# Activation tiles moved 64 bytes against the weight tiles in a transformer kernel of one core

## The chip, the core and the metric

The kernel runs on one core of one Trainium2 chip. The time is the time on the device in microseconds (us), from the runs of the whole program; lower is better. The profile is one further execution, taken by the hardware profiler, with its own time. TensorE (PE in the rows) multiplies: it loads a stationary operand of up to 128 columns (PEld in the rows) and streams a moving operand past it. VectorE is DVE, ScalarE is ACT, GpSimd is POOL, and SyncE (SP) issues most of the DMAs. SBUF is the on-chip memory that TensorE reads both operands from; an address below is the byte in each of its 128 partitions at which a tile starts.

## What is computed

Two transformer models one after the other on 256 tokens of width 1024. The first is a block of a mixer (gated delta rule and a state-space layer), a cross attention and a gated feed-forward; the second has two layers, each of a self attention, a small cross attention on a memory, and a feed-forward with a short convolution. Cut to the feed-forward of the first block and the rule of every projection:

```python
def _swiglu(hn, w_gate, w_up, w_down):
    return (jax.nn.silu(hn @ w_gate) * (hn @ w_up)) @ w_down

def conv_ffn(h, w_up, conv_w, conv_b, w_down):
    u = h @ w_up                                  # [256, 2 * 2816]
    ...
    return (jax.nn.silu(gate) * val) @ w_down

def reference(...):
    x = first_block(x, mem, ...)
    return second_block(x, mem_2, positions_2, ...)
```

All inputs are float32, and each of the 1024-wide weight matrices is used once.

## The kernel before

**The products.** A float32 product is made of three products in the format fp32r: each operand is split into a high part and a low part, and the kernel adds high x high, high x low and low x high. `mm3` (lines 533 to 536) does this for the projections, `out_mm` (lines 574 to 582) for the products that add into the residual. In `proj_f` the stationary operand is a 128x128 piece of the weights (`whi`, `wlo`) and the moving one 256 columns of the activations (`xh`, `xl`); in `proj_t` (lines 545 to 553) the two change sides. In `out_mm` the weights are stationary and `oh`, `ol` or the two halves of `ahl` move. So every matmul of these lines has a weight load of 128 columns and a moving operand of 256 columns, both of 4 bytes.

**Weights on their way.** `Weights` (lines 45 to 185) loads 512 KB of a matrix at a time on the SP queue (line 101) into a `raw` tile. ScalarE copies it to `whi` (line 137), VectorE subtracts to get `wlo` (line 157), and the load that comes next may then use the `raw` tile. There are four `raw` tiles and four pairs of `whi`, `wlo` in the pool `weights`, three more pairs in the pool `weights2`, which is opened at line 1682, and from line 1685 on two extra load tiles (`raw4`) in the pool `main`. Of 336 loads of line 101, 136 land in `raw4`.

**Where the tiles lie.** Pools are placed one behind the other, and the tiles of a pool one behind the other, each rounded up to 32 bytes. In the built program before the change the order is `const`, `weights` (from byte 7808), `main` (from 56960), `small`, then `mixer` and later `second` in its place (from 119296), and `weights2` (from 196352). All of `weights`, `main` and `weights2` and nearly all tiles of `second` start at a multiple of 128: `whi` and `wlo` of `weights` at 128 past a multiple of 256, those of `weights2` at a multiple of 256, `xh` (69248) and `xl` (77440) at 128 past one, `ahl`, `oh` and `ol` at a multiple of 256. Every step inside these tiles from one matmul to the next is a multiple of 512 bytes. A few tiles lie elsewhere: in `mixer`, the tile `s5ghl` (the gated state-space output, high and low half, from 139200) lies 64 past a multiple of 128, and it moves past `whi` and `wlo` in 48 matmuls of lines 534 to 536; in `second`, `wfs` (from 190656, the 16 gate columns of the second layer, high and low) also lies 64 past one, and it is stationary for `xh` and `xl` in 16 matmuls of lines 564 and 565.

**The order.** The kernel is written with tile pools and a scheduler that fixes each engine's order when the program is built. TensorE works through its matmuls in that order, and the weight load of one matmul runs while the matmul ahead of it streams.

Of the kernel before, what the change touches and what calls it, by code (L numbers as in the profile page):

```python
# [10 lines left out]
F32 = mybir.dt.float32  # L11
# [176 lines left out]
def behind(tc, later, earlier):  # L188

    tc.add_manual_dep(later, earlier.name, mybir.DependencyInfo(  # L190
        mybir.DependencyClass.NoSync, mybir.DependencyReason.DATA), reason="order")
# [38 lines left out]
def body(ctx, tc, I, out):  # L230
# [7 lines left out]
    main = ctx.enter_context(tc.tile_pool(name="main", bufs=1))  # L238
    small = ctx.enter_context(tc.tile_pool(name="small", bufs=2))
    W = Weights(nc, wpool, 4, 4, lambda a, b: behind(tc, a, b))  # L240


    def cols(w, c0, c1):
        return w.rearrange("(k p) n -> p k n", p=128)[:, :, c0:c1]

    def rows(w, r0, n=2):
        return w[r0 * 128:(r0 + n) * 128].rearrange("(k p) n -> p k n", p=128)
# [3 lines left out]
    for nm in "ukqvz":  # L251
        for c in range(2):
            W.add((nm, c), cols(w_in, OFFS[nm] + 256 * c, OFFS[nm] + 256 * c + 256), split=nm not in "uk")
            for x, at in enumerate(XK_AT):
                if at == (nm, c):
                    W.add(("xk", x), cols(I["w_xk"][0], 256 * x, 256 * x + 256))
    W.add("glu", I["s5_w_glu"][0].rearrange("(k p) n -> p k n", p=128), "k")
    for c in (2, 3, 0, 1):
        W.add(("out", c), rows(I["w_out"][0], 2 * c), "k")
    for i in range(4):  # L260
        W.add(("xq", i), cols(I["w_xq"][0], 256 * i, 256 * i + 256), order=False)
        W.add(("xv", i), cols(I["w_xv"][0], 256 * i, 256 * i + 256), "k", order=False)
        W.add(("xo", i), rows(I["w_xo"][0], 2 * i), "k", order=False)
# [1416 lines left out]
    residual(accs, COL["ffn"])  # L1680
    px_cm.__exit__(None, None, None)
    W.more = (ctx.enter_context(tc.tile_pool(name="weights2", bufs=1)), 3)
    padded = ctx.enter_context(tc.tile_pool(name="padded", bufs=1))
    W.nextra = 2
    W.extra = lambda: main.tile([128, 2048], F32, name="raw4", tag="m8", bufs=3)
# [496 lines left out]
```

## Time and profile before

| | |
|---|---|
| median of 3 runs | 1225.01 us |
| lowest and highest of them | 1219.74 and 1227.4 us |
| the profiled execution's own time | 1218.84 us |
| its span, first to last instruction | 1217.1 us |
| mean granted TensorE clock | 0.99 of full speed |
| TensorE matmuls busy | 1180.5 us (97%), 9720 instructions |
| TensorE weight loads busy | 1127.1 us (93%), 9720 |
| VectorE, ScalarE, GpSimd busy | 893.4, 667.1, 77.6 us |

A matmul's busy time runs from its start to a modelled end, and the next one starts before that end, so busy time adds up overlaps. What one matmul costs in a stream is the time from its start to the start of the next; it is read from the rows of the timeline.

### The profile page before, as it was taken

To read this page: it belongs to the slowest core of one execution; us is meant where nothing else is said; L and a number is where in the kernel's file an instruction comes from. 1 tells how busy PE (TensorE), PEld (TensorE's weight loads), DVE (VectorE), ACT (ScalarE), POOL (GpSimd) and SP (SyncE) were. 2 spreads that over 40 slices of the span, in tenths; PEclk is the share of its full clock that TensorE was granted. 3 is DMA by queue.
4 is the path that set the end of the run, shared out by engine and by line. 5 is a ranking of instruction groups with operands and counts; after the bars stand their busy time and mean duration, and the time that the engine had idled before them with its cause. 6 is when DMAs were issued, how large, how long until landed. Compare 5 with 4: busy or idle time off the path is not lost.

```text
span 1217.1 us, 24101 instructions
## 1 busy us (share of the span) xinstructions
PE 1180.5 (97%) x9720; PEld 1127.1 (93%) x9720; DVE 893.4 (73%) x1682; ACT 667.1 (55%) x1155; POOL 77.6 (6%) x175
## 2 busy tenths in 40 slices
PE   7899998999999999999998999999999999999998
PEld 6799888999999999997897999999988888999998
DVE  8799747766775656787776888777665676977775
ACT  5554345755544444655666665555454666655553
POOL 1426300100000000300000000000100000000000
PEclk9999899999999999999999999999999999999998
DMA  8733353647655655743352665765543454566520
GB/s 211 187 93 104 87 161 107 184 152 194 192 177 175 206 174 148 219 144 121 112 158 90 187 179 174 211 188 156 140 139 117 145 158 135 174 188 193 174 87 35
DMA packets 262017, 188.01 MB, mean 154 GB/s; under 512 B 20143, under 2 KB 246852, under 8 KB 261906
## 3 DMA queue, kind: packets, MB, share of 16 engines
q1 hardware_dynamic: 258034, 185.23, 51.4%
q8 instruction: 76, 1.25, 0.4%
q10 hardware_dynamic: 3568, 0.86, 0.3%
q0 software_dynamic: 304, 0.39, 0.3%
q14 instruction: 35, 0.29, 0.1%
HBM read 183.70 MB, written 2.75 MB: 153 GB/s over the span
## 4 chain that ended last, share of the span: by engine, by line
PE 88%; DVE 4%; DMA 3%; ACT 2%; issue 1%; POOL 1%; SPq 0%; ACTq 0%; DVEq 0%; POOLq 0%
PE mm L534 17%; PE mm L535 17%; PE mm L536 17%; PE acc L580 7%; PE acc L582 7%; PE acc L581 7%; PE mm L1377 2%; DMA raw<-in_w_in_dram 1%; PE acc L1991 1%; PE acc L1862 1%; DMA D<-d 1%; DVE wlo L157 1%; DMA raws<-in_w_out_dram 1%; PE mm L2045 1%; PE mm L1578 0%
## 5 line engine op out<-in xcount | busy, mean ns | idle before, releaser
L137 ACT ACTIVATE whi<-raw 128x1024 fp32r<-128x1024 f32 x322 | 337.1, 1057 | 319.0 <-PE mm L535 114.8
L157 DVE TENSOR_TENSOR wlo<-raw,whi 128x1024 fp32r<-128x1024 f32 x322 | 392.4, 1227 | 162.0 <-ACT whi L137 159.7
L534 PE MATMUL mm<-xh,whi 128*128 128x256 f32 x1504 | 427.0, 285 | 2.1 <-ACT V L218 1.2
L535 PE MATMUL mm<-xl,whi 128*128 128x256 f32 x1504 | 425.7, 283 | 0.0
L536 PE MATMUL mm<-xh,wlo 128*128 128x256 f32 x1504 | 425.4, 283 | 0.0
L534 PEld LDWEIGHTS mm<-xh,whi 128*128 128x128 f32 x1504 | 286.3, 191 | 4.2 <-ACT V L218 1.4
L535 PEld LDWEIGHTS mm<-xl,whi 128*128 128x128 f32 x1504 | 286.7, 191 | 1.4 <-issue 1.1
L536 PEld LDWEIGHTS mm<-xh,wlo 128*128 128x128 f32 x1504 | 286.8, 191 | 0.3
L582 PE MATMUL acc<-ahl,wlo 128*128 128x256 f32 x528 | 146.4, 282 | 0.4 <-DVE wlo L157 0.4
L581 PE MATMUL acc<-ahl,whi 128*128 128x256 f32 x528 | 146.4, 282 | 0.0
L580 PE MATMUL acc<-ahl,whi 128*128 128x256 f32 x528 | 143.3, 282 | 0.0
L582 PEld LDWEIGHTS acc<-ahl,wlo 128*128 128x128 f32 x528 | 99.2, 189 | 0.7 <-DVE wlo L157 0.6
L581 PEld LDWEIGHTS acc<-ahl,whi 128*128 128x128 f32 x528 | 99.4, 189 | 0.0
L580 PEld LDWEIGHTS acc<-ahl,whi 128*128 128x128 f32 x528 | 97.3, 189 | 0.3 <-ACT ahl L218 0.2
L1736 DVE SCALAR_TENSOR_TENSOR gu<-pad,cwc,gu 128x256 f32<-128x256 f32 x176 | 75.3, 480 | 3.4 <-ACT gu L218 3.4
L580 PE MATMUL acc<-oh,whi 128*128 128x256 f32 x224 | 62.5, 288 | 0.9 <-ACT oh L218 0.9
L582 PE MATMUL acc<-oh,wlo 128*128 128x256 f32 x224 | 62.8, 283 | 0.0
L581 PE MATMUL acc<-ol,whi 128*128 128x256 f32 x224 | 62.5, 281 | 0.0
L218 ACT ACTIVATE gu<-pad,cwc 128x256 f32<-128x256 f32 x88 | 47.5, 589 | 13.9 <-DVE pad L745 13.9
L745 DVE TENSOR_TENSOR pad<-mm,rb 128x512 f32<-128x512 f32 x44 | 30.2, 689 | 20.1 <-PE mm L536 20.1
L580 PEld LDWEIGHTS acc<-oh,whi 128*128 128x128 f32 x224 | 41.3, 188 | 2.5 <-ACT oh L218 1.9
L582 PEld LDWEIGHTS acc<-oh,wlo 128*128 128x128 f32 x224 | 42.1, 188 | 1.1 <-issue 1.1
(537 smaller groups left out, 1962.7 us busy)
## 6 DMA issues: line engine op xcount, KB each, us to landing
raw<-in_ffn_w_up_dram SPq DMA_DIRECT2D x88, 512.0 KB
raw<-in_ffn_w_down_dram SPq DMA_DIRECT2D x44, 512.0 KB
raw<-in_ab_w_in_dram SPq DMA_DIRECT2D x24, 512.0 KB
raw<-in_fox_w_in_dram SPq DMA_DIRECT2D x24, 512.0 KB
raw<-in_w_gate_dram SPq DMA_DIRECT2D x22, 512.0 KB
raw<-in_w_up_dram SPq DMA_DIRECT2D x22, 512.0 KB
raw<-in_w_down_dram SPq DMA_DIRECT2D x22, 512.0 KB
raw<-in_w_in_dram SPq DMA_DIRECT2D x20, 512.0 KB
```

Source lines behind the costliest of these rows:

```text
L137: i_ = self.nc.scalar.activation(hi, src, AF.Copy)
L157: i_ = self.nc.vector.tensor_tensor(lo, src, hi.bitcast(F32), op=OP.subtract)
L218: i = self.nc.scalar.activation(out, in_, func, **kw)
L534: T.matmul(p, lhsT=wh, rhs=xh, start=start, stop=False, **kw)
L535: T.matmul(p, lhsT=wh, rhs=xl, start=False, stop=False, **kw)
L536: T.matmul(p, lhsT=wl, rhs=xh, start=False, stop=stop, **kw)
L580: T.matmul(p, lhsT=wh[:, kk, c], rhs=xh, start=first and n % 2 == 0, stop=False, skip_group_check=True)
L581: T.matmul(p, lhsT=wh[:, kk, c], rhs=xl, start=False, stop=False, skip_group_check=True)
L582: T.matmul(p, lhsT=wl[:, kk, c], rhs=xh, start=False, stop=last, skip_group_check=True)
L745: N.v = V.tensor_tensor(o, a, b, op=op).ins
L1377: T.matmul(p, lhsT=w[:, k], rhs=x32[:, k], start=k == 0, stop=k == KD - 1)
L1736: STT(t[:, i], u[:, i, d:d + S], cw(d, j + NH * i), t[:, i], op0=OP.mult, op1=OP.add)
```

## The change

Two tiles of 16 float32 columns (64 bytes in each partition) are allocated and never used: one at the head of the pool `main`, one at the head of `weights2`.

```diff
     W = Weights(nc, wpool, 4, 4, lambda a, b: behind(tc, a, b))
+
+    main.tile([128, 16], F32, name="beside", bufs=1)
 
...
     W.more = (ctx.enter_context(tc.tile_pool(name="weights2", bufs=1)), 3)
+    W.more[0].tile([128, 16], F32, name="beside2", bufs=1)
     padded = ctx.enter_context(tc.tile_pool(name="padded", bufs=1))
```

The first moves every tile that is allocated behind it by 64 bytes: all of `main` (from 57024 now), `small`, `mixer`, `second`, `cross`. The pool `weights` lies ahead of it and stays. `weights2` would be moved by 64 too; the second tile moves its `whi` and `wlo` by 64 more, so that they start at multiples of 128 again (128 past a multiple of 256 now). In the built program `xh` and `xl` start 192 past a multiple of 256, `ahl`, `oh` and `ol` 64 past one, and all `whi` and `wlo` 128 past one: each pair of lines 534 to 536 and 580 to 582 is 64 bytes apart, counted in multiples of 128. The pairs that were 64 apart come to the same place, like `s5ghl` with `whi`; `wfs` moves with `main`'s tiles and stays 64 apart from them. The tiles `raw` stay, `raw4` moves by 64. Each engine's instructions, their order and what each waits for are the same in both programs, line by line.

## Rows read from the trace of the kernel before

**Rows 1.** The page: busy us of each engine, and the chain that ended last.
```profile
span 1217.1 us, 24101 instructions
...
PE 1180.5 (97%) x9720; PEld 1127.1 (93%) x9720; DVE 893.4 (73%) x1682; ACT 667.1 (55%) x1155; POOL 77.6 (6%) x175
...
PE 88%; DVE 4%; DMA 3%; ACT 2%; issue 1%; POOL 1%; SPq 0%; ACTq 0%; DVEq 0%; POOLq 0%
```

**Rows 2.** Busy us (instructions) by stretch; then granted clock, DMA share, GB/s.
```profile
400.00:500.00 100.00, 100.00 (x838) 99.85 (x838) 63.26 (x81) 51.63 (x73) 1.57 (x1) 1.00 0.62 180
700.00:800.00 100.00, 100.00 (x840) 100.00 (x839) 83.08 (x128) 57.66 (x88) 0.93 (x1) 1.00 0.63 186
1100.00:1200.00 100.00, 100.00 (x838) 99.86 (x838) 75.05 (x118) 54.06 (x81) 0.00 (x0) 1.00 0.42 127
```

**Rows 3.** Groups by line, PE: form, count, busy us, mean ns, idle before.
```profile
L534 PE MATMUL mm<-xh,whi 128*128 128x256 f32 x1504 | 427.0, 285 | 2.1 <-ACT V L218 1.2 <-ACT xh L218 0.9
...
L581 PE MATMUL acc<-ahl,whi 128*128 128x256 f32 x528 | 146.4, 282 | 0.0
...
L581 PE MATMUL acc<-ol,whi 128*128 128x256 f32 x224 | 62.5, 281 | 0.0
...
L536 PE MATMUL mm<-whi,xl 128*128 128x256 f32 x128 | 37.0, 289 | 0.0
...
L534 PE MATMUL spare<-memh,whi 128*128 128x256 f32 x64 | 19.5, 304 | 2.4 <-ACT xkT L218 2.4
...
L581 PE MATMUL dn<-xl,whi 128*128 128x256 f32 x32 | 9.0, 283 | 0.0
```

**Rows 4.** Timeline of PE, 301.60 to 303.04 us: start us, duration us, instruction.
```profile
301.60 0.28 PE L534 MATMUL mm<-xh,whi 128*128 128x256 f32 x1
301.72 0.28 PE L535 MATMUL mm<-xl,whi 128*128 128x256 f32 x1
...
303.04 0.28 PE L534 MATMUL mm<-xh,whi 128*128 128x256 f32 x1
```

**Rows 5.** Timeline of PEld, the weight loads, at the same place; columns as in Rows 4.
```profile
301.60 0.19 PEld L535 LDWEIGHTS mm<-xl,whi 128*128 128x128 f32 x1
```

**Rows 6.** Groups by line in that stretch; columns as in Rows 3.
```profile
L534 PEld LDWEIGHTS mm<-xh,whi 128*128 128x128 f32 x5 | 1.0, 192 | 0.0
```

**Rows 7.** Timeline of PE, 750.92 to 753.66 us, 24 matmuls of the down projection.
```profile
750.92 0.28 PE L580 MATMUL acc<-ahl,whi 128*128 128x256 f32 x1
...
751.63 0.28 PE L580 MATMUL acc<-ahl,whi 128*128 128x256 f32 x1
751.76 0.28 PE L581 MATMUL acc<-ahl,whi 128*128 128x256 f32 x1
...
753.66 0.28 PE L582 MATMUL acc<-ahl,wlo 128*128 128x256 f32 x1
```

**Rows 8.** Timeline of PE, 178.63 to 182.28 us, 32 matmuls.
```profile
178.63 0.28 PE L535 MATMUL mm<-s5ghl,whi 128*128 128x256 f32 x1
...
182.28 0.28 PE L535 MATMUL mm<-s5ghl,whi 128*128 128x256 f32 x1
```

**Rows 9.** Timeline of PE, 184.83 to 186.08 us, 12 matmuls.
```profile
184.83 0.28 PE L535 MATMUL mm<-s5ghl,whi 128*128 128x256 f32 x1
...
186.08 0.28 PE L580 MATMUL s<-xh,whi 128*128 128x256 f32 x1
```

**Rows 10.** Timeline of PE, 871.45 to 873.05 us, 15 matmuls.
```profile
871.45 0.28 PE L565 MATMUL acc<-xl,wfs 128*16 128x256 f32 x1
...
871.80 0.28 PE L564 MATMUL acc<-xh,wfs 128*32 128x256 f32 x1
...
873.05 0.28 PE L565 MATMUL acc<-xl,wfs 128*16 128x256 f32 x1
```

**Rows 11.** The tile s5ghl: ns min/median/max, first and last start us.
```profile
L534 PEld LDWEIGHTS mm<-s5ghl,whi x16: 187/188/192, 178.2 to 185.6; 128*128 128x128 f32 x16
...
L218 ACT ACTIVATE s5ghl<-s5g x4: 406/407/408, 177.1 to 178.1; 128x256 fp32r<-128x256 f32 x4
L745 DVE TENSOR_TENSOR s5ghl<-s5g,s5ghl x4: 418/420/425, 177.6 to 178.6; 128x256 fp32r<-128x256 f32 x4
```

**Rows 12.** The tile ahl, the same columns.
```profile
L218 ACT ACTIVATE ahl<-sl x66: 398/401/420, 326.3 to 1198.8; 128x256 fp32r<-128x256 f32 x66
L745 DVE TENSOR_TENSOR ahl<-sl,ahl x66: 415/420/428, 327.5 to 1199.2; 128x256 fp32r<-128x256 f32 x66
```

**Rows 13.** Clock and DMA in the four stretches; columns as in Rows 2.
```profile
178.70:182.30 3.60, 3.60 (x33) 3.60 (x32) 2.21 (x4) 2.00 (x5) 0.00 (x0) 1.00 0.14 19
184.90:186.00 1.10, 1.10 (x12) 1.10 (x12) 0.88 (x3) 1.10 (x3) 0.00 (x0) 1.00 0.00 0
301.60:303.00 1.40, 1.40 (x14) 1.40 (x13) 1.40 (x5) 1.15 (x4) 0.00 (x0) 1.00 0.85 202
871.80:873.00 1.20, 1.20 (x13) 1.07 (x11) 1.17 (x3) 0.00 (x0) 0.00 (x0) 1.00 1.00 329
```

## The prediction

> **What bounds the kernel now.** I read the page first, then the stretches, then single starts. The page [rows 1] shows TensorE busy for 97% of 1217.1 us, and the chain that ended last runs on it for 88%. VectorE is busy for 73%. In three stretches of 100 us out of the feed-forwards TensorE and its weight loads are both busy for all of the time, at full clock, and 838 to 840 matmuls pass in each [rows 2]: one starts 119.3 ns behind the other. VectorE is at 63 to 83% there and the DMA engines at 42 to 63%, so what bounds these stretches is the pace of TensorE itself, and whatever changes that pace changes the time nearly one for one.
>
> So the number to look at is the time from start to start. A projection out of `xh` [rows 4] starts a matmul every 1.44 us / 12 = 120.0 ns. The weight load of the next matmul starts together with it [rows 5] and takes 192 ns [rows 6]. A down projection [rows 7] has 23 steps in 2.74 us, 119.1 ns each, but unevenly: one of them, at 751.63, is 130 ns wide at the timeline's resolution of 10 ns.
>
> Now the same triple of products with `s5ghl` as the moving operand. It has the same form, 256 columns past 128, and the same kind of weights; but `s5ghl` lies 64 bytes beside a multiple of 128 from `whi` and `wlo`, where `xh` and `ahl` lie at a multiple of 128 from them. One stream of it [rows 8] makes 31 steps in 3.65 us, 117.7 ns each. Another, 2.5 us later [rows 9], makes 11 steps in 1.25 us, 113.6 ns each. In the third stream of such pairs, `xh` and `xl` past `wfs` [rows 10], the first three steps take 117 ns (871.45 to 871.80), and the following 11 take 1.25 us again, 113.6 ns each. The weight loads of `s5ghl` take 188 ns at the median [rows 11] against 192. The clock is full in all of these stretches [rows 13]. The DMA engines stand still in the one at 184.9 us and are full in the one at 871.8 us, at the same pace; so the pace does not follow the traffic. What the streams below 118 ns share is the 64 bytes.
>
> **The change part by part.** No instruction comes, goes or moves, so the whole effect is in durations.
>
> *TensorE.* The pairs that change sides are those of lines 534 to 536 and 580 to 582. Counted from rows [rows 3], each line standing for the three of its triple: 3 x 1504 of `xh`, 3 x 528 of `ahl`, 3 x 224 of `oh`, 3 x 128 with the sides exchanged, twice 3 x 64 with `memh` (once with the sides exchanged), and four times 3 x 32 of `mem2h` and of the last projection of the mixer: 4512 + 1584 + 672 + 384 + 384 + 384 = 7920. Their cost now is 119.3 ns a step [rows 2], 945 us together. Their cost behind the change is not in the trace of before, because none of these streams lies 64 apart; the nearest rows are the three streams that do. They bound it: at 113.6 ns each step saves 5.7 ns, 7920 x 5.7 = 45 us; at 117.7 ns it saves 1.6 ns, 7920 x 1.6 = 13 us. Both paces hold for ten steps and more, in one and the same form, and I see nothing in the rows that says which of them a stream falls into. By streams it is two to one for the fast pace; by steps (31 and 3 to 22) it is three to two for the slow one. I take the middle, 115.6 ns: 7920 x 3.7 = 29 us.
>
> *The other way.* The 48 matmuls of `s5ghl` come to a multiple of 128 from their weights. At 120.0 ns against a mean near 116 they lose 48 x 4 ns = 0.2 us. `wfs` keeps its 64 bytes.
>
> *VectorE and ScalarE.* They read and write the moved tiles too. The same two operations on `s5ghl` (64 beside) take 407 and 420 ns at the median [rows 11], on `ahl` (a multiple of 128) 401 and 420 ns [rows 12]. I put nothing down for them; 6 ns on each ScalarE copy would lie beside TensorE's work, since ScalarE is at 52 to 58% [rows 2].
>
> *Cover.* A faster TensorE asks for weights sooner. At 113.6 ns the 100 us stretches last 95 us; VectorE's 83.1 us are then 87% and the DMA share of 0.63 becomes 0.66. The DMA engines have shown a share of 0.85 beside a TensorE that didn't wait [rows 13], so the cover holds, and I take nothing off.
>
> **The sum.** 1218.84 - 29 + 0.2 = 1190 us, from the profiled execution's own time. That execution lies 6 us below the median of the runs, 1225.01; a median of the changed kernel may lie as much above my number.
>
> **The rivals.**
>
> *A, all in the fast pace.* Every stream falls into 113.6 ns as in [rows 9, 10]: 1218.84 - 45 = 1174 us. For it: in [rows 10] the stream goes from the slower pace to the faster and stays. Against: [rows 8] stays slow for 31 steps.
>
> *B, all in the slow pace.* 117.7 ns everywhere: 1206 us. For it: that is the longest of the three streams, and most like the projections. Against: the two others.
>
> *C, no change.* The three streams are faster for a reason of their own, or the place of an operand has no effect. [...] The time would then be 1219 us. What the rows have against it is 192 against 188 ns for a load and 120.0 against 113.6 ns for a step in the same form [rows 4, 6, 9, 11]; what they leave open is whether the 64 bytes did it, for three streams are few. One thing speaks for it: the unevenness of [rows 7] shows that the pace also varies where the distance is a multiple of 128.
>
> *D, slower.* The two readings meet later instead of at the start: with one operand half of 128 bytes ahead, the load catches up with the matmul inside it, and the streams settle at the wide steps that [rows 7] has now and then, say 122 to 125 ns. 7920 x 2.7 to 5.7 ns is 21 to 45 us: 1240 to 1264 us. It decides once the mean step is above 120.8 ns (1% of the time is 12 us, and 12 / 7920 is 1.5 ns). Against it: no pace in [rows 8 to 10] is above 118 ns.
>
> The moved load tiles `raw4` could be written more slowly. The DMA engines would bind only if the share of 0.63 grew to 1, that is, if these 40% of the loads took 2.5 times as long. [...]
>
> **How the numbers follow.** The mixture of both paces: 0.42. A: 0.20. B: 0.15. C: 0.17. D: 0.06. A measurement of this kernel tells about 1% from no change, which is 12 us. Faster by more than that are the mixture, A, and most of B (1206 is 19 us below the median, 13 below the profiled time): 0.42 + 0.20 + 0.13 = 0.75. Within 1%: C and the rest of B, 0.19. Slower: D, 0.06. The range reaches from A at its lower bound with a few us of scatter, 1168, to C at the median of the runs, 1225; it leaves out D and half of C, and a little of A. The likeliest case's own range, with 114.5 to 117 ns a step, is 1180 to 1202.
>
> **What would show it.** The step in the projections, 120.0 ns now, should lie between 113 and 118 ns, and the weight loads of `xh` should take 188 ns instead of 192. The 100 us stretches should hold 850 to 880 matmuls instead of 838. The streams of `s5ghl` should go up to about 120 ns. VectorE's and ScalarE's durations should stay, and their shares rise by the shortening alone. If steps and loads stay at 120 and 192 ns, C holds. If the step falls and the time does not, waits of TensorE for `wlo`, `whi` or `raw` must have grown, and my cover was wrong.

## The result and the profile of the changed kernel

The changed kernel takes 1208.34 us (median of 4 runs, 1203.32 to 1209.01) against 1222.85 us for the kernel before, measured beside it: a ratio of 0.987, with a 95% interval of 0.983 to 0.991. So it is faster, by half of the forecast gain: 14.5 us between the medians and 15.5 us between the profiled executions (1203.32 against 1218.84), where 29 us were forecast.

The page of the changed kernel: its span, the busy us of each engine, and the chain that ended last; these answer to [rows 1].

```profile
span 1201.5 us, 24101 instructions
...
PE 1163.9 (97%) x9720; PEld 1110.1 (92%) x9720; DVE 890.5 (74%) x1682; ACT 667.5 (56%) x1155; POOL 79.5 (7%) x175
...
PE 86%; DVE 5%; DMA 4%; ACT 3%; POOL 1%; issue 1%; SPq 0%; DVEq 0%; ACTq 0%; POOLq 0%
```

TensorE is still the bound, with 16.6 us less of busy time; VectorE's and ScalarE's busy times are within 3 us of those before. The same three stretches as [rows 2], busy us and instructions of PE, PEld, DVE, ACT and POOL, then granted clock, DMA share and GB/s:

```profile
400.00:500.00 100.00, 99.89 (x859) 99.70 (x858) 66.38 (x81) 52.23 (x76) 5.47 (x4) 1.00 0.63 183
700.00:800.00 100.00, 100.00 (x852) 100.00 (x851) 82.68 (x128) 57.96 (x87) 0.93 (x1) 1.00 0.66 189
1100.00:1200.00 100.00, 95.33 (x813) 94.92 (x811) 72.32 (x125) 50.82 (x79) 0.00 (x0) 1.00 0.37 113
```

838 to 840 matmuls have become 852 to 859 (the third stretch now holds the end of the program). Single starts, PE's timeline of the changed kernel at four places (start us, duration us, instruction): a projection out of `xh`, a down projection of the first feed-forward, one of the second, and the stream of `s5ghl`, which the change brought from 64 to 128 bytes past its weights, counted modulo 256 (it starts at byte 139264 now, a multiple of 256, and `whi` at 128 past one).

```profile
338.87 0.28 PE L536 MATMUL mm<-xh,whi 128*128 128x256 f32 x1
...
341.70 0.28 PE L536 MATMUL mm<-xh,whi 128*128 128x256 f32 x1
```

```profile
337.51 0.28 PE L582 MATMUL acc<-ahl,whi 128*128 128x256 f32 x1
...
338.76 0.28 PE L584 MATMUL acc<-ahl,wlo 128*128 128x256 f32 x1
```

```profile
744.60 0.28 PE L584 MATMUL acc<-ahl,wlo 128*128 128x256 f32 x1
...
747.07 0.28 PE L584 MATMUL acc<-ahl,wlo 128*128 128x256 f32 x1
```

```profile
180.48 0.28 PE L536 MATMUL mm<-s5ghl,whi 128*128 128x256 f32 x1
...
182.86 0.28 PE L538 MATMUL mm<-s5ghl,wlo 128*128 128x256 f32 x1
```

The projection makes 24 steps in 2.83 us, 117.9 ns each, where [rows 4] had 120.0. The first down projection makes 11 steps in 1.25 us, 113.6 ns (the timeline rounds to 10 ns; by the trace's starts in whole ns, streams of this pace go at 113.3); the one of the second feed-forward, with the same operands at the same places, 21 steps in 2.47 us, 117.6 ns. `s5ghl` went from 117.7 [rows 8] to 119.0 ns (20 steps in 2.38 us), unevenly, like the down projection of [rows 7], which was 128 apart. So both paces that the prediction had seen are there, and the frequent one is the slow one. The weight loads of the projections went from 192 [rows 6] to 188 ns, and the two operations that make the weights kept their time: 1226 ns against 1227 before, and 1057 in both (page, groups by line: form, count, busy us, mean ns, idle before and its releaser):

```profile
L157 DVE TENSOR_TENSOR wlo<-raw,whi 128x1024 fp32r<-128x1024 f32 x322 | 391.9, 1226 | 151.1 <-ACT whi L137 149.3
L137 ACT ACTIVATE whi<-raw 128x1024 fp32r<-128x1024 f32 x322 | 337.1, 1057 | 299.7 <-PE mm L537 117.3
...
L536 PEld LDWEIGHTS mm<-xh,whi 128*128 128x128 f32 x1504 | 281.8, 188 | 4.2 <-ACT V L218 1.4
```

**Where the time went.** Below, a *step* is the time from the start of an fp32r matmul of 256 columns to the start of the next, where that is below 135 ns (nothing waited). Summed over the trace, before has 7910 steps with a mean of 119.36 ns, 944.2 us; the changed kernel 7904 with 117.06, 925.2 us. Matched one to one, the steps got 18.1 us shorter, and all other time of TensorE 1.8 us longer, 3.4 us of it in the mixer between 117 and 198 us, where the granted clock of the stretch from 100 to 150 us was 0.86 instead of 0.90.

### The profile page after: what moved, and what is told of

It is laid out like the page before. It is cut to its first block, busy times and chain, and to the rows that moved or that the text cites. A ratio compares the mean times of both kernels' runs of the same rounds, so it can differ in the third digit from the quotient of the medians.

```text
span 1201.5 us, 24101 instructions
## 1 busy us (share of the span) xinstructions
PE 1163.9 (97%) x9720; PEld 1110.1 (92%) x9720; DVE 890.5 (74%) x1682; ACT 667.5 (56%) x1155; POOL 79.5 (7%) x175
## 3 DMA queue, kind: packets, MB, share of 16 engines
q8 instruction: 76, 1.25, 0.4%
## 4 chain that ended last, share of the span: by engine, by line
PE 86%; DVE 5%; DMA 4%; ACT 3%; POOL 1%; issue 1%; SPq 0%; DVEq 0%; ACTq 0%; POOLq 0%
PE mm L536 17%; PE mm L537 17%; PE mm L538 17%; PE acc L584 7%; PE acc L582 7%; PE acc L583 7%; DMA raw<-in_w_in_dram 1%; PE acc L1994 1%; DVE wlo L157 1%; PE acc L1865 1%; DMA D<-d 1%; ACT whi L137 1%; DMA raws<-in_w_out_dram 1%; DMA s5u<-uT 1%; PE mm L2048 1%
## 5 line engine op out<-in xcount | busy, mean ns | idle before, releaser
L157 DVE TENSOR_TENSOR wlo<-raw,whi 128x1024 fp32r<-128x1024 f32 x322 | 391.9, 1226 | 151.1 <-ACT whi L137 149.3
L137 ACT ACTIVATE whi<-raw 128x1024 fp32r<-128x1024 f32 x322 | 337.1, 1057 | 299.7 <-PE mm L537 117.3
L536 PE MATMUL mm<-xh,whi 128*128 128x256 f32 x1504 | 422.5, 282 | 2.2 <-ACT V L218 1.2
L537 PE MATMUL mm<-xl,whi 128*128 128x256 f32 x1504 | 421.0, 280 | 0.0
L538 PE MATMUL mm<-xh,wlo 128*128 128x256 f32 x1504 | 420.3, 280 | 0.0
L536 PEld LDWEIGHTS mm<-xh,whi 128*128 128x128 f32 x1504 | 281.8, 188 | 4.2 <-ACT V L218 1.4
L537 PEld LDWEIGHTS mm<-xl,whi 128*128 128x128 f32 x1504 | 281.9, 188 | 1.4 <-issue 1.1
L538 PEld LDWEIGHTS mm<-xh,wlo 128*128 128x128 f32 x1504 | 282.2, 188 | 0.3
L583 PE MATMUL acc<-ahl,whi 128*128 128x256 f32 x528 | 145.1, 279 | 0.0
L582 PE MATMUL acc<-ahl,whi 128*128 128x256 f32 x528 | 141.7, 279 | 0.0
L747 DVE TENSOR_TENSOR pad<-mm,rb 128x512 f32<-128x512 f32 x44 | 30.1, 688 | 18.2 <-PE mm L538 18.1
```

The source lines that it names most:

```text
L137: i_ = self.nc.scalar.activation(hi, src, AF.Copy)
L157: i_ = self.nc.vector.tensor_tensor(lo, src, hi.bitcast(F32), op=OP.subtract)
L536: T.matmul(p, lhsT=wh, rhs=xh, start=start, stop=False, **kw)
L537: T.matmul(p, lhsT=wh, rhs=xl, start=False, stop=False, **kw)
L538: T.matmul(p, lhsT=wl, rhs=xh, start=False, stop=stop, **kw)
L582: T.matmul(p, lhsT=wh[:, kk, c], rhs=xh, start=first and n % 2 == 0, stop=False, skip_group_check=True)
```

## The experiments

The number that orders them is the *distance*: the start of the moving operand, minus the start of the stationary operand that is loaded while it streams (that of the matmul behind), modulo 256. A *pair* is such a moving operand and such a load. Before, `xh` lies at 0 and `ahl`, `oh` at 128 from the weights of the first pool, and the reverse from those of `weights2`. In the changed kernel `xh` lies at 64 and `ahl`, `oh` at 192 everywhere, and nearly all of the few streams in which weights move past activations at 192. All kernels down to the last four below have the instructions, the order and the waits of the kernel before; only the places of the tiles differ. Their edits are given against the kernel before.

### Is it the distance?

Two kernels. The first moves everything, weights too, by 64 bytes; the second moves the activations by 128.

```diff
+    wpool.tile([128, 16], F32, name="beside0", bufs=1)     # e_all64, ahead of the weights
+    main.tile([128, 32], F32, name="beside", bufs=1)       # e_main128, instead
```

> The 64-byte tile stands ahead of the weight tiles, so weights and activations both move by 64 bytes and every distance between the two operands of a matmul is that of the kernel before. Theory 1 (the distance of the two operands sets the step from one matmul to the next): no change, about 1222 us, steps of 120.0 ns in the projections out of xh, loads of 192 ns. Theory 2 (the place of the activations itself, or the moved load tiles, sets it): about 1208 us and steps of 117.7 ns as in the changed kernel.

> Activations moved by 128 bytes instead of 64. xh and xl then lie 128 past a multiple of 256 from the weights, where the down and output projections (ahl, oh) lie now, and these lie at a multiple of 256, where xh lies now. Theory 1a (only the distance within 128 bytes counts): no change, 1222 us. Theory 1b (the distance within 256 bytes counts): the two groups change paces, xh from 119.8 to about 118.5 ns a step and ahl and oh from 118.7 to about 120 ns; 5200 x -1.3 + 2200 x 1.3 ns is -4 us, 1218 us.

Measured: e_all64 1222.58 us, ratio 1.0007 (0.9989 to 1.0025); e_main128 1219.4 us, 0.9959 (0.994 to 0.9978). The stretch from 700 to 800 us, of e_all64 and of e_main128:

```profile
700.00:800.00 100.00, 100.00 (x840) 100.00 (x839) 83.14 (x130) 57.39 (x88) 0.93 (x1) 1.00 0.63 184
```

```profile
700.00:800.00 100.00, 100.00 (x842) 100.00 (x842) 83.42 (x128) 58.17 (x87) 0.93 (x1) 1.00 0.62 190
```

With everything 64 bytes on, but the distances as before, 840 matmuls pass, as in [rows 2]. With `xh` and `ahl` exchanging their distances, they exchange their paces: `xh` at 128 goes unevenly at a mean of 118.74 ns (4604 steps), and a down projection now runs in steps of 120.0, eight of them in 0.96 us, where [rows 7] was uneven at 119.1. PE's timeline of e_main128:

```profile
744.83 0.28 PE L581 MATMUL acc<-ahl,whi 128*128 128x256 f32 x1
...
745.79 0.28 PE L583 MATMUL acc<-ahl,wlo 128*128 128x256 f32 x1
```

So in these two kernels the step went with the distance, not with the place (840 matmuls in the stretch of e_all64, as before) and not with the stream's identity; and 128 is too small a modulus, since `xh` went at 119.79 ns at 0 (before) and at 118.74 ns at 128.

### Which distance

```diff
+    main.tile([128, 48], F32, name="beside", bufs=1)       # e_main192: xh 192, ahl and oh 64 (first pool only)
+    main.tile([128, 8], F32, name="beside", bufs=1)        # e_main32: xh 32, ahl and oh 160
+    W.more[0].tile([128, 24], F32, name="beside2", bufs=1)
+    main.tile([128, 24], F32, name="beside", bufs=1)       # e_main96: xh 96, ahl and oh 224
+    W.more[0].tile([128, 8], F32, name="beside2", bufs=1)
```

> Activations moved by 192 bytes: 64 apart from the weights of the first pool again, but to the other side. In the changed kernel the moving operand lies 64 past the weights in the projections out of xh (steps of 117.7 ns) and 64 ahead of them, in 256 bytes, in the down and output projections (115.9 ns). Here the sides are exchanged. Theory A (the side sets the pace): xh about 115.9 ns and ahl, oh about 117.7 ns a step; against the changed kernel 4000 x -1.8 + 2000 x 1.8 ns, about -4 us, 1204 us less what the second weight pool loses (its pairs lie as in the kernel before: 900 x 1.5 ns, +1 us). Theory B (both sides hold two paces, 117.7 and 113.3 ns, and what enters the stream decides): xh keeps 117.7 ns where it comes from a slow stream; 1208 us.

> Activations moved by 32 bytes, the second weight pool with them so that all weights lie alike: xh 32 past the weights, ahl and oh 160 past (32 past a multiple of 128). Theory 1 with a step at 64 bytes (two places count as one within 64 bytes): as the kernel before, 1222 us, xh at 120 ns. Theory 1 in small steps: half of the gain, xh near 118.8 ns, about 1214 us.

> xh and xl 96 past a multiple of 256 from their weights in both pools, ahl and oh at 224, the exchanged streams at 160. Measured so far: 32 gave 116.8 ns (xh), 64 117.7, 128 118.7, 160 119.0 (ahl) and 118.3 (oh), 192 115.4 to 116.0, 224 118.4 (exchanged), 0 119.8. Theory 1 (a curve that rises from 32 to 160 and has its low point at 192): xh at 118.2, ahl at 118.4, 7900 steps at a mean of 118.2 ns, 9 us less than before: 1210 us profiled. Rival 2 (multiples of 64 alone are special, and 32 and 96 are alike): xh at 116.8, 1203 us.

Measured: e_main192 1202.68 us, ratio 0.9836 (0.9811 to 0.9862); e_main32 1213.49 us, 0.9918 (0.989 to 0.9945); e_main96 1222.52 us, 0.9998 (0.9982 to 1.0015). In e_main192 the two groups exchange the mean paces of the changed kernel, as its theory A had it. The 1214 us that one theory gave e_main32 came out by luck: `xh` went to 116.8 ns where it said 118.8, and `ahl` and `oh`, at 160, hardly got faster. The means of the large groups, from the starts in each trace:

| distance | stream (kernel) | steps | mean ns | at most 114.5 ns |
|---|---|---|---|---|
| 0 | xh (before) | 3978 | 119.79 | 1% |
| 32 | xh (e_main32) | 4576 | 116.81 | 10% |
| 64 | xh (changed kernel) | 4605 | 117.70 | 3% |
| 64 | ahl (e_main192) | 1311 | 117.87 | 1% |
| 96 | xh (e_main96) | 4589 | 119.89 | 0% |
| 128 | ahl (before) | 1311 | 118.81 | 1% |
| 160 | ahl (e_main32) | 1573 | 118.99 | 0% |
| 192 | ahl (changed kernel) | 1573 | 116.00 | 39% |
| 192 | xh (e_main192) | 3955 | 115.43 | 53% |
| 224 | ahl (e_main96) | 1573 | 118.24 | 0% |

The curve that was expected for e_main96 is wrong, and so is its rival: 96 is as slow as 0, and 32 isn't like 96. At 32 the steps are uneven: one stream makes 14 of them in 1.63 us, and the trace's starts in whole ns show 117, 120, 114 and 116 ns again and again, 116.75 at the mean (PE's timeline of e_main32):

```profile
345.33 0.28 PE L536 MATMUL mm<-xl,whi 128*128 128x256 f32 x1
...
346.96 0.28 PE L535 MATMUL mm<-xh,whi 128*128 128x256 f32 x1
```

Of the eight distances of the table, only at 64 and 192 was a stream seen at about 113 ns step after step (11 steps at 64 in [rows 9]; at 192, 11 steps of the first down projection above). Two further kernels ask whether 64 and 192 are two things, or whether what was fast at 192 was fast for another reason: e_both64 puts every stream to 64, and e_shift128 keeps the changed kernel's distances and moves all tiles, weights too, by another 128 bytes, so that each operand's own place modulo 256 is exchanged. (These and all that follow free 256 bytes by a smaller reserve for DMA descriptors.)

```diff
+    main.tile([128, 16], F32, name="beside", bufs=1)       # e_both64
+    pm.tile([128, 32], F32, name="beside1", bufs=1)        #   at the head of the pool second
+    W.more[0].tile([128, 48], F32, name="beside2", bufs=1)
+    wpool.tile([128, 32], F32, name="beside0", bufs=1)     # e_shift128
+    main.tile([128, 16], F32, name="beside", bufs=1)
+    W.more[0].tile([128, 16], F32, name="beside2", bufs=1)
```

> The mirror: every moving tile lies 64 past a multiple of 256 from its weights, in both pools; the streams with the sides exchanged at 192. Theory 1 (64 and 192 are different, and 64 mostly keeps 117.7 ns): xh as in the changed kernel at 117.7 ns, ahl up from 116.0 to 117.9, oh from 115.4 to 116.4 or more, the exchanged ones at 115.8: 1573 x 1.9 + 633 x 1.0 = 3.6 us more than the changed kernel, 1207 us for a profiled run, a mean step of 117.5 ns. Rival 2 (which stream it is decides, not the side): ahl and oh stay at 116.0 and 115.4, 1203 us.

> The changed kernel with all of its tiles, weights too, 128 further on: each distance as in the changed kernel, but the weights at a multiple of 256 instead of 128 past one, xh at 64 past one instead of 192, ahl at 192 instead of 64. Theory 1 (only the distance counts): xh at 117.7 ns, ahl at 116.0, the same time as the changed kernel, 1203 to 1208 us. Rival 2 (the place of the moving operand modulo 256 decides: in the runs so far the fast streams were those whose moving operand lay at 64 past a multiple of 256): xh becomes fast, 115.4 ns, ahl slow, 117.9; 4605 x 2.3 - 1573 x 1.9 = 7.6 us less, 1196 to 1200 us.

Measured: e_both64 1207.96 us, ratio 0.9877 (0.9843 to 0.9911); e_shift128 1202.25 us, 0.9831 (0.981 to 0.9853). The first feed-forward, 70 us out of it, in the changed kernel, in e_shift128 and in e_both64:

```profile
400.00:470.00 70.00, 70.00 (x604) 70.00 (x603) 41.86 (x50) 31.41 (x41) 0.00 (x0) 1.00 0.65 190
```

```profile
400.00:470.00 70.00, 70.00 (x604) 70.00 (x603) 42.22 (x50) 31.55 (x42) 0.00 (x0) 1.00 0.62 189
```

```profile
400.00:470.00 70.00, 70.00 (x597) 70.00 (x596) 41.77 (x50) 31.01 (x42) 0.00 (x0) 1.00 0.64 187
```

e_shift128 repeats the changed kernel to the matmul: 604 and 604 here, `xh` at a mean of 117.70 ns in both, `ahl` at 116.00 in both. So again the step went with the distance alone. In e_both64 `ahl` is slow throughout (117.79 ns, none at 113.3) and the first feed-forward loses its fast down projections, as theory 1 had it; the time is that of the changed kernel within the intervals.

What the two also show is that a choice between the paces can repeat. In the changed kernel a down projection that follows an up projection without a pause took the fast pace in 17 of 19 cases in the first feed-forward, in 0 of 21 in the second and 1 of 21 in the third; in e_shift128 the counts are the same three. The traces also show what fits this, where streams at 192, 64 and 192 followed each other without a wait. The stretch at 64 went at 117.75 ns out of either pace, and yet the stream behind it mostly took up the pace that the one ahead of it had: in the traces of the changed kernel, e_main192, e_shift128 and e_reset_no0 (below), fast to fast 46 times, slow to slow 84 times, slow to fast 3 times, and never fast to slow (stretches of six steps and more, most of them turns of the same loops). So a down projection mostly had the pace of the one before it.

### What chooses between 113.3 and 117.75 ns

The next kernel puts all moving tiles at 192 and leaves no change of distance between up and down projections.

```diff
+    main.tile([128, 48], F32, name="beside", bufs=1)       # e_all192
+    pm.tile([128, 32], F32, name="beside1", bufs=1)
+    W.more[0].tile([128, 16], F32, name="beside2", bufs=1)
```

> Every moving tile (xh, xl, ahl, oh, ol, mem) lies 192 past a multiple of 256 from its weights, in both weight pools; the streams with the sides exchanged then lie at 64. The profiled kernel with only the pairs on the first pool at 192 for xh and 64 for ahl had xh steps of 115.43 ns, and the changed kernel had ahl steps of 116.0 and oh steps of 115.44 ns at 192. Theory 1 (the distance modulo 256 sets which paces a stream may take, and at 192 it falls into 113.3 ns about half of the time): all big classes at 115.4 to 116 ns, 7900 steps at a mean of 115.6, 11 us less than the changed kernel's profiled 1203.3: 1192 us, and no more than a few us given back. Rival 2 (the pace depends on the stretch of the program and its loads, and some streams will run slowly wherever the operands lie): a mean near that of the best so far, 116.4 ns, 1200 us. Rival 3 (a faster TensorE now runs into its loads): steps of 115.6 ns, but more idle time before the first matmul of a stream, 1200 us or more.

Measured: 1201.85 us, ratio 0.9819 (0.9795 to 0.9844). The mean step is 116.05 ns (7903 steps), between theory 1 and rival 2; all other time of TensorE grew by 3.7 us against before, so rival 3 is not what is missing. But the mean hides the finding. Three stretches, one out of each feed-forward:

```profile
400.00:470.00 70.00, 70.00 (x620) 70.00 (x620) 43.75 (x52) 32.20 (x43) 0.00 (x0) 1.00 0.66 196
700.00:800.00 100.00, 100.00 (x852) 100.00 (x851) 81.67 (x124) 56.59 (x84) 0.93 (x1) 1.00 0.64 192
1050.00:1150.00 100.00, 100.00 (x851) 100.00 (x850) 77.14 (x119) 57.32 (x84) 0.00 (x0) 1.00 0.60 179
```

The first feed-forward runs wholly at 113 ns (70 us / 620), the other two wholly at 117.4 (100 us / 852). In the first, 1221 matmuls in a row keep the fast pace; in the third, 1374 keep the slow one. Where the third became slow can be seen: twelve steps at 113.3 ns (1.36 us), then the broadcast of the statistics of line 455, a plain float32 matmul that stands in the trace as two records, 0.59 us together, and from there ten steps of 118 ns (1.18 us). PE's timeline of e_all192:

```profile
1014.33 0.28 PE L535 MATMUL mm<-xh,whi 128*128 128x256 f32 x1
...
1015.69 0.28 PE L535 MATMUL mm<-xh,whi 128*128 128x256 f32 x1
1015.80 0.59 PE L455 MATMUL acc<-diag,ones 128*128 128x256 f32 x2
1016.05 0.47 PE L536 MATMUL mm<-xl,whi 128*128 128x256 f32 x1
1016.35 0.28 PE L537 MATMUL mm<-xh,wlo 128*128 128x256 f32 x1
...
1017.53 0.28 PE L535 MATMUL mm<-xh,whi 128*128 128x256 f32 x1
```

So in this trace a pace held over more than a thousand matmuls (1221 and 1374), and at this one matmul of another form it changed. To test whether an interruption sets the pace and the stream then keeps it, the same kernel gets nine matmuls in the second and third feed-forward, whose result is overwritten by the projection behind them. In e_kick9 they have the sides exchanged, which makes their distance 64, with one pair at 0 on the way in (`xh` streams while `xh` is loaded) and one on the way out (`whi` while `whi` is loaded); in e_kick9_same they are like the projections. The two kernels differ in these rows alone.

```diff
             p = mm()
+            if conv is not None and j == 4:
+                wh, _ = W.get((tag, "g", j // 2), j % 2)
+                for _ in range(9):
+                    T.matmul(p[:, :S], lhsT=N.xh[:, 0, 0:128], rhs=wh[:, 0:2].rearrange("p k c -> p (k c)"), start=True, stop=True)    # e_kick9
+                    T.matmul(p[:, :S], lhsT=wh[:, 0], rhs=N.xh[:, 0], start=True, stop=True)    # e_kick9_same
             proj_f(p[:, :S], (tag, "g", j // 2), j % 2)
```

> The kernel with every moving tile at 192 past its weights, plus nine matmuls each in the feed-forwards of the second model's two layers, ahead of the fifth gate projection, with the sides exchanged (weights move, activations stand: distance 64), whose result the next projection overwrites. Without them the trace shows both feed-forwards in the 117.75 ns pace, 1405 steps from 662.0 to 829.4 us and 1345 from 1020.0 to 1178.9 us, set by the statistics matmuls at their head. Theory 1 (the pace is a state that an entry sets and that holds until something breaks the stream; in the six cases of that kernel where weights had moved at 64 in the 117.75 pace and activations came back at 192, the stream went on at 113.3): behind the nine matmuls the steps fall to 113.3 ns and stay: some 2650 steps x 4.4 ns = 11.7 us, less 18 x 0.118 = 2.1 us for the added matmuls: about 9.5 us less than without, 1186 us profiled, median about 1192. Rival 2 (the pace belongs to the stretch, its loads and its neighbours): 117.75 ns stays, 2 us more, median 1204.

> The same nine matmuls at the same two places, with the sides as in the projections (weights stand, activations move: distance 192); all else, the order of every engine too, is that of the kernel with the exchanged sides. Theory 1 (only a change of the distance disturbs the state): the stretches stay at 117.75 ns, 2 us more than without the matmuls, median 1204. Rival 2 (any added matmuls, or the shifted order around them, change the pace): the same gain as with the exchanged sides, about 1192.

Measured: e_kick9 1199.66 us, ratio 0.9793 (0.9758 to 0.9828); e_kick9_same 1202.15 us, 0.9827 (0.9796 to 0.9857). By the times alone this would have been a failure of theory 1, which expected 10 us between them. The traces say otherwise. The second feed-forward of e_kick9 around the nine matmuls (line 1761):

```profile
674.37 0.28 PE L536 MATMUL mm<-xl,whi 128*128 128x256 f32 x1
...
675.54 0.28 PE L537 MATMUL mm<-xh,wlo 128*128 128x256 f32 x1
675.66 1.22 PE L1761 MATMUL mm<-whi,xh 128*128 128x256 f32 x9
...
677.08 0.28 PE L535 MATMUL mm<-xh,whi 128*128 128x256 f32 x1
...
679.34 0.28 PE L537 MATMUL mm<-xh,wlo 128*128 128x256 f32 x1
```

Ten steps of 117 ns ahead of them (1.17 us), twenty of 113 behind (2.26 us), and this goes on for 1329 matmuls. In the third feed-forward of the same execution the statistics had, this time, left the stream in the fast pace, and the nine matmuls turned it slow:

```profile
1021.00 0.28 PE L536 MATMUL mm<-xl,whi 128*128 128x256 f32 x1
...
1022.13 0.28 PE L537 MATMUL mm<-xh,wlo 128*128 128x256 f32 x1
1022.24 1.19 PE L1761 MATMUL mm<-whi,xh 128*128 128x256 f32 x9
1023.26 0.28 PE L535 MATMUL mm<-xh,whi 128*128 128x256 f32 x1
...
1024.91 0.28 PE L537 MATMUL mm<-xh,wlo 128*128 128x256 f32 x1
```

113 ns ahead (1.13 us / 10), 117.9 behind (1.65 us / 14), for 1332 matmuls. In e_kick9_same the second feed-forward came in slow and the third fast, and both stayed so. One stretch out of each feed-forward of e_kick9, then of e_kick9_same:

```profile
400.00:470.00 70.00, 70.00 (x620) 70.00 (x620) 43.45 (x52) 32.42 (x45) 0.00 (x0) 1.00 0.66 197
700.00:800.00 100.00, 100.00 (x885) 100.00 (x884) 84.40 (x129) 59.31 (x88) 0.93 (x1) 1.00 0.65 191
1050.00:1150.00 100.00, 100.00 (x852) 100.00 (x851) 78.03 (x119) 56.30 (x82) 0.00 (x0) 1.00 0.60 179
```

```profile
400.00:470.00 70.00, 70.00 (x597) 70.00 (x596) 42.17 (x51) 31.52 (x42) 0.00 (x0) 1.00 0.63 191
700.00:800.00 100.00, 100.00 (x851) 100.00 (x850) 82.41 (x126) 56.99 (x84) 0.93 (x1) 1.00 0.64 185
1050.00:1150.00 100.00, 100.00 (x884) 100.00 (x884) 79.86 (x124) 58.96 (x86) 0.00 (x0) 1.00 0.62 185
```

Of the two feed-forwards with added matmuls, each kernel has one fast and one slow, the other way round, so these two cancel. The first feed-forward has none, and the two programs are the same up to there; it ran fast in e_kick9 and slow in e_kick9_same. So behind the same instructions the pace was fast in one execution and slow in the other (620 and 597 matmuls in 70 us). Matched one to one, the steps of e_kick9 are 2.5 us shorter in all (means of 115.54 and 115.86 ns), which is why the times are close. Theory 1 holds in that a pace went on once it was there (1329 and 1332 matmuls behind the nine), but its guess that the exchanged sides always lead to the fast pace falls: in these two cases they exchanged the two. That may be why the runs of e_kick9 spread from 1191.6 to 1203.0 us; no trace shows each of them.

The transitions in the traces of five kernels (changed, e_main192, e_both64, e_shift128, e_all192) offer a way that doesn't depend on the pace at entry. Where both paces can be read, every step from distance 192 straight to 64 ended at 117.75 ns, 97 times out of the slow pace and 53 times out of the fast one; and from 64 in the slow pace, over one pair at distance 0, to 192, it went on at 113.3 ns in 20 of 26 cases. (From 192 over one pair at 0 to 64, as in e_kick9, streams kept their pace, 12 fast and 13 slow.) e_reset does both in a row in all three feed-forwards; e_reset_no0 leaves the pair at 0 out.

```diff
             p = mm()
+            if j == (6 if conv is None else 4):
+                wh, _ = W.get((tag, "g", j // 2), j % 2)
+                for at in [32] * 8 + [16] * 1:              # e_reset; [32] * 9 in e_reset_no0
+                    T.matmul(p[:, :S], lhsT=wh[:, 0], rhs=N.xh.rearrange("p k s -> p (k s)")[:, at:at + S], start=True, stop=True)
             proj_f(p[:, :S], (tag, "g", j // 2), j % 2)
```

> The kernel with every moving tile at 192, and nine added matmuls in each of the three feed-forwards, whose result the next projection overwrites: weights stand as in the projections, and the activations move from 128 bytes further on in eight of them (distance 64) and from 64 bytes further on in the last (distance 0). So far the exchanged sides turned the 117.75 pace into 113.3 (1329 steps) in one feed-forward and 113.3 into 117.75 (1332 steps) in the other. In the traces so far every step from 192 to 64 without a pair at 0 between ended in the 117.75 pace, whichever it came from (about 160 cases), and of the steps from 64 in that pace over a pair at 0 to 192, 20 of 26 went on at 113.3. Theory 1 (the pace is a state, and these transitions set it, whatever it was): all three feed-forwards at 113.3 ns behind the added matmuls; against the kernel without them, 2650 steps x 4.4 = 11.7 us less where that was slow, plus 27 x 0.118 = 3.2 us: about 1189 us profiled, median 1193. Rival 2 (the nine matmuls leave the state as it came in, or by chance): one or two of the three at 117.75, median 1197 to 1204.

> The same, but all nine added matmuls at distance 64, so that the stream goes from 64 to 192 without a pair at 0 between. In the traces so far that step went both ways: down projections behind up projections 36 to 113.3 and 74 to 117.75. Theory 1 (the transition sets the pace): the state behind the nine matmuls may be either, but it follows one rule: the first steps read 116, 116, 114 where it becomes fast and 114, 119, 117 where it stays slow, and it holds until the next disturbance. In two of three feed-forwards slow: median 1200 to 1204. Rival 2 (the pair at 0 doesn't matter): the same time as with it, 1193.

Measured: e_reset **1189.96 us**, ratio 0.9728 (0.9706 to 0.9749); e_reset_no0 1197.03 us, 0.9796 (0.9768 to 0.9823). The three stretches of e_reset, and then of e_reset_no0:

```profile
400.00:470.00 70.00, 70.00 (x620) 70.00 (x619) 43.32 (x52) 32.41 (x44) 0.00 (x0) 1.00 0.66 197
700.00:800.00 100.00, 100.00 (x884) 100.00 (x884) 84.27 (x130) 59.97 (x88) 0.93 (x1) 1.00 0.66 194
1050.00:1150.00 100.00, 100.00 (x885) 100.00 (x884) 79.37 (x122) 58.41 (x85) 0.00 (x0) 1.00 0.62 186
```

```profile
400.00:470.00 70.00, 70.00 (x620) 70.00 (x619) 43.78 (x52) 32.17 (x43) 0.00 (x0) 1.00 0.66 196
700.00:800.00 100.00, 100.00 (x852) 100.00 (x851) 81.39 (x124) 56.54 (x83) 0.93 (x1) 1.00 0.62 186
1050.00:1150.00 100.00, 100.00 (x885) 100.00 (x884) 78.99 (x123) 58.85 (x86) 0.00 (x0) 1.00 0.62 187
```

In e_reset all three run at 113 ns behind the nine matmuls; they came in slow, slow and fast. Three places in one trace are few; the other four runs of e_reset took no longer than this one, but no trace shows them. Without the pair at 0 the second stayed slow and the first and third were fast, "either", as theory 1 had allowed, where rival 2 expected the same time. All three had gone through the nine matmuls at 117.8 to 118.2 ns a step, also the two that had come in fast, and each left as it had come, like the streams at 192, 64 and 192 above. The two profiled executions themselves hardly differ, 1194.13 and 1193.41 us: matched one to one, e_reset's steps are 6.4 us shorter and all other time of TensorE 7.9 us longer, and the granted clock from 100 to 250 us, ahead of all added matmuls, was 0.93 against 0.98. The medians differ by 7 us. e_reset is 18.4 us below the changed kernel by the medians (of different jobs, where the kernel before took 1221.20 and 1222.85 us), with 27 matmuls (3.2 us) more, and it is the best kernel here.

## Why the prediction was right in its direction and too large

- **What bounds the kernel** was right: steps that are shorter by 18.1 us made the execution shorter by 15.5 us, nearly one for one.
- **That the 64 bytes set the pace** was right, though argued from three streams, of which only the two of `s5ghl` have the form of the rest: the loads of [rows 10] have 16 and 32 columns, not 128. The controls e_all64 and e_shift128 keep each pace when everything moves together, and `s5ghl`, now 128 from its weights, went to 119.0 ns, near the forecast 120. The prediction counted modulo 128; the runs show that 0 and 128 differ (119.79 and 118.74 ns for `xh`), so 128 is too small.
- **The term that failed is 7920 x 3.7 ns.** Its count was right (7904 steps, where nothing waited, were measured), its price was not: half of the way from the slow pace to the fast one was forecast for every step, and the step came to 117.06 ns instead of 115.6, so that the term measured 18.1 us instead of 29. By streams: `xh` was forecast at 115.6 and came to 117.70, 4605 x 1.9 ns = 8.8 us of gain where the term had 4605 x 3.7 = 17.0 us; `ahl` at 116.00 and `oh` at 115.44 came close to it. The middle between two paces was taken because nothing in the rows said which of them a stream takes; that was true of the rows of before, but a middle is the likeliest value only if the large streams mix. `xh`, 58% of the steps, doesn't: 96% of its steps at 64 lie at 116 to 119 ns.
- **Which rival it was.** The time, 1208.34 us, is nearest to B (all at 117.7 ns, 1206), which had 0.15; by mechanism it is the mixture, `xh` slow and part of `ahl` and `oh` fast. The range of 1168 to 1225 held it, the likeliest case's own range of 1180 to 1202 did not.
- **Rival C** (no change) did not come. Before and changed kernel differ in no instruction, and yet a weight load of `xh` took 192 ns at the median in one and 188 in the other, and a step 119.4 and 117.1 ns at the mean. Here, where both operands have four bytes an element, the step went with the distance between them. Why is not shown.
- **Rival D** (about 122 to 125 ns at 64) did not come at 64 or 192. Steps of 125 ns are frequent at distance 96 alone, 739 of 4589 (e_main96). That two readings meet was the author's guess; no run shows it.
- **Cover** held. In e_reset's second feed-forward VectorE is at 84% and the DMA share at 0.66, with TensorE busy for all of the time; the prediction had 87% and 0.66 for that pace. The 1.8 us that were given back lie in the mixer, not in the feed-forwards.
- **VectorE and ScalarE** kept their durations: 1226 and 1057 ns (1227 and 1057 before), and 418 and 401 ns on `ahl` (420 and 401 before, [rows 12]).

## What to carry to other kernels

When a stream of matmuls is bound by its own pace, look at the step from start to start by the places of the operands: here the start of the moving operand against that of the weights loaded meanwhile, modulo 256, was worth up to 5.6% of a step (120.0 against 113.3 ns), and it can be changed by an unused tile. When the rows show two paces for one form, don't forecast their mean: find out what chooses between them, or give the time of each its own chance. Where the program was the same, up to the second feed-forward of e_kick9 and e_kick9_same, the pace of the first one still differed, 620 matmuls in 70 us against 597; so read the pace in each trace. And where kernels with equal times are compared, count matmuls by stretch, for one fast and one slow part can cancel.

## What the runs showed of the hardware

- The steps of one and the same pair, fp32r, a load of 128 columns and a moving operand of 256, took 120.0 ns at distance 0 (before), 117.75 or 113.3 ns at 64 and 192 (changed kernel, e_main192, e_all192), an uneven 113 to 120 ns at 32 (e_main32, 116.81 at the mean), and an uneven 115 to 125 ns at 96, 128, 160 and 224 (e_main96, before, e_main32, e_main96: 119.89, 118.81, 118.99 and 118.24 at the mean). Why is not shown.
- At 192 two paces lasted: the slow one for 1374 matmuls, 162 us, the fast one for 1221 (e_all192). In e_kick9 the slow one went over into the fast one at nine matmuls, eight pairs at 64 with one at 0 on either side, for the 1329 that followed (117 ns ahead, 113 behind).
- The pace of the moment did not tell the next one: a stretch at 64 between two at 192 went at 117.75 ns, and behind it the pace of before came back in 130 of 133 cases (changed kernel, e_main192, e_shift128, e_reset_no0).
- Behind the same interruption the pace was not always the same. The third feed-forward was slow behind the statistics matmul in e_all192 (118 ns) and fast in e_kick9 (113 ns), and the first feed-forward of e_kick9 and e_kick9_same, the same program up to there, ran fast in one and slow in the other (620 and 597 matmuls in 70 us). What decides it stays open: no run here varied it. That the down projections of the first feed-forward are fast and those of the others slow, in the changed kernel and e_shift128 alike (17 of 19 fast, against 0 of 21 and 1 of 21), fits the pace of the first of them carried on.
- What is left: even in e_reset the mean step is 114.7 ns: 113.3 in the parts of the feed-forwards behind the added matmuls, 116.0 in all others, where no added matmul stands.
